# Small products of a two-block transformer kernel, redone: modulation sums, gates, stick-breaking sums, masks and the convolution's norm

## The chip, the cores and the metric

The kernel runs on one core of one Trainium2 chip, in one launch. The metric is the device time of one execution in microseconds (us); lower is better. The median of three runs of the kernel before is 2573.98 us (2573.61 to 2575.96).

The names of the engines below: PE is the matrix engine (PEld its weight loads, which overlap its products), DVE the vector engine, ACT the scalar engine, POOL the general-purpose engine whose queue also issues DMAs, SP the engine whose queue issues the weight loads from DRAM.

## The reference, cut to what matters

256 tokens, width 2048, float32. A first block has two layers: a stick-breaking attention of 16 heads, and a latent attention of 16 heads with a mask by chunks of 64 tokens; each is followed by a per-layer embedding with a gate. A second block is modulated by a vector `c`: a convolution branch with a layer norm, a sparse attention that picks keys, and a feed-forward part of width 5632.

```python
# stick-breaking attention, per head: z [queries, keys]
log_keep = jnp.where(strict, jax.nn.log_sigmoid(-z), 0.0)
later = lax.cumsum(log_keep, axis=3, reverse=True) - log_keep
w = jnp.where(strict, jnp.exp(jax.nn.log_sigmoid(z) + later), 0.0)

# latent attention, per head
s = jnp.where(kchunk[None, :] <= qchunk[:, None], s, NEG_INF)

# second block
mod = silu(c) @ w_ada + b_ada                     # [2048] @ [2048, 12288]
sh1, sc1, gt1, sh2, sc2, gt2 = jnp.split(mod, 6)
x = x + gt1 * rms_norm_2(mixed, g_post_mix)       # later gt2 with g_post_ffn
# in the convolution branch, over 1024 features of each token
y = (xf - mu) * lax.rsqrt(var + EPS)
```

## The kernel before

**The main stream.** Nearly all work is `act @ w` for 256 tokens. The weights come from DRAM in pieces of 512 KB (`Run.load`, tile `wst`, four of them, SP's queue). `Run.consume` splits each piece into two float32r parts, `wh` on ACT (L148) and `wl` on DVE (L149), in a ring of six. `Run.go` then emits, chunk by chunk, three float32r products into `acc` or `sc` (L268 to L270), most of them 512 columns wide. A unit is one piece against one half of the tokens: 6 products of 512 columns.

**Side work.** Everything else is written as generators. After each unit `Run.side` advances those that are due; `yield n` means "n units later". Each engine takes its instructions in the order in which this one program emits them, so the numbers behind `yield` set how far ahead of the matrix engine the other engines get a step. Behind the side work of a unit, `Run.pump` emits the split of the next pieces, at most ten units ahead of their use and only as ring slots are given back by PE.

**Modulation.** `w_ada` is 2048 x 12288. It comes as 384 chunks of 128 x 512 (tile `ast`, three of them, POOL's queue, L245), spread over the whole program. DVE multiplies each by a column of `silu(c)` and adds it to an accumulator `ada` [128, 512] (L421, L424). When 16 chunks are in, `ada_sum` adds up the 128 partitions: four float32 products with a column of ones, one per 128 columns (L435), which put the sums straight into four columns of `tp`; DVE adds the bias into `mods` (L438). There are 24 such sums. A float32 product shows as two passes in the trace, so one sum is 8 passes.

**Gates.** `times_gate` makes gate rows on all partitions: for each of 16 blocks of 128 columns a float32 product of a broadcast column with the identity (L452), and DVE multiplies a row of gains by it (L455). It runs at the start of the mix's output projection (`begin_m`) and, in four pieces, behind the last sum.

**Stick-breaking head.** `stick_head` emits the scores `z` with two float32 products and two masks (bf16 identity times `stick`, 128 columns each), then |z|, exp, ln on ACT and `sp = softplus(z)` on DVE (L646). Three units later three float32 products with triangular or all -1 matrices form the cumulative sums (256, 128 and 128 columns, L634, 6 passes), ACT takes exp into `w`, and two units later the products with `v` follow. All products of this function carry the line L634, that of its helper `mm`.

**Latent head.** `mla_head` (products at L984) adds two bf16 masks of 128 columns, one between the float32 products and one behind them.

**Convolution's norm.** `conv_norm` sums 1024 features per token with a matrix of 1/1024: eight float32 products of 256 columns for the mean (L1165) and, after squares on ACT, eight for the variance (L1179), the latter in four visits.

## Time and profile before

| | |
|---|---|
| median of three runs | 2573.98 us (2573.61 to 2575.96) |
| span of the profiled execution, first to last instruction | 2573.5 us |
| profiled execution's own time | not given apart from the span; the median lies 0.5 us above the span |
| PE busy | 2530.5 us, 98% of the span |
| DVE busy | 1689.0 us, 66% |
| ACT busy | 1262.0 us, 49% |
| POOL busy | 291.8 us, 11% |
| DMA | 562.39 MB, mean 219 GB/s |

A matrix product's record is longer than the time that it takes from the engine, since products are pipelined: the time it takes is the distance from its start to the next one's start. In a timeline an entry with x8 merges eight records, and the next entry's start minus its own is what all eight take. "Idle before" names what released an engine. In the view of waits a row reads: engine, tile and line that waited, the engine, tile and line (or DMA) that ended it, then total us, times, longest.

### The profile page before, as it was taken

What the parts mean: (1) busy time and instruction counts of PE and PEld (TensorE: products, weight loads), DVE (VectorE), ACT (ScalarE), POOL (GpSimd) and SP (SyncE); (2) the same over time, 40 slices, a digit from 0 to 9 for tenths busy, and PEclk for the clock granted to TensorE, in tenths of its full rate; (3) what the DMA queues carried; (4) which work ended last, traced back from release to release, by engine and by line L of the source; (5) the groups of instructions that cost most, each with busy time, mean ns of one, the idle gap of its engine ahead of it and who ended that gap; (6) DMA issues with size and microseconds to landing.
All of it is one profiled execution on the core that took longest, in us unless ns stands there. A gap on an engine that the chain in (4) does not pass through costs nothing.

```text
span 2573.5 us, 33331 instructions
## 1 busy us (share of the span) xinstructions
PE 2530.5 (98%) x12127; PEld 2101.4 (82%) x12127; DVE 1689.0 (66%) x2304; ACT 1262.0 (49%) x1814; POOL 291.8 (11%) x561
## 2 busy tenths in 40 slices
PE   8999999999999999999999999999999999999998
PEld 6888888878889978878877877888788888888886
DVE  6666667677775566668889756676765555645545
ACT  6544464455656545554444554445544444334443
POOL 2111112111313310000000001110100100100000
PEclk9999999999999999999999999999999999999999
DMA  8777768867886566655655535875577777756553
GB/s 266 248 254 250 237 227 283 286 199 247 283 285 191 188 227 208 222 191 174 188 160 168 172 138 181 279 281 197 185 263 232 237 234 233 246 181 188 192 192 127
DMA packets 271844, 562.39 MB, mean 219 GB/s; under 512 B 20800, under 2 KB 43584, under 8 KB 269632
## 3 DMA queue, kind: packets, MB, share of 16 engines
q1 hardware_dynamic: 237264, 439.61, 52.7%
q0 software_dynamic: 34384, 120.65, 13.5%
q8 instruction: 95, 1.56, 0.2%
q14 instruction: 69, 0.57, 0.1%
q10 hardware_dynamic: 32, 0.01, 0.0%
HBM read 551.79 MB, written 8.39 MB: 218 GB/s over the span
## 4 chain that ended last, share of the span: by engine, by line
PE 93%; DVE 4%; ACT 2%; issue 1%; DMA 1%; POOL 0%; DVEq 0%; POOLq 0%; ACTq 0%; SPq 0%
PE acc L268 21%; PE acc L270 21%; PE acc L269 21%; PE sc L268 7%; PE sc L270 7%; PE sc L269 7%; PE tp L363 1%; DVE wl L149 1%; PE sc L634 1%; PE sc L984 1%; PE tp L435 1%; PE sc L1274 1%; PE sc L1240 1%; PE pv L1274 0%; PE tp L610 0%
## 5 line engine op out<-in xcount | busy, mean ns | idle before, releaser
L149 DVE TENSOR_TENSOR wl<-wst,wh 128x1024 fp32r<-128x1024 f32 (+3 forms) x794 | 949.4, 1199 | 628.7 <-ACT wh L148 627.0
L148 ACT ACTIVATE wh<-wst 128x1024 fp32r<-128x1024 f32 (+3 forms) x794 | 822.5, 1039 | 852.5 <-PE sc L270 491.2
L268 PE MATMUL acc<-wh,ah 128*128 128x512 f32 (+4 forms) x1934 | 761.5, 394 | 7.7 <-ACT wh L148 3.7
L269 PE MATMUL acc<-wl,ah 128*128 128x512 f32 (+4 forms) x1934 | 744.6, 385 | 0.9 <-DVE wl L149 0.9
L270 PE MATMUL acc<-wh,al 128*128 128x512 f32 (+4 forms) x1934 | 744.9, 385 | 0.0
L268 PEld LDWEIGHTS acc<-wh,ah 128*128 128x128 f32 x1934 | 365.1, 189 | 81.5 <-issue 6.7
L270 PEld LDWEIGHTS acc<-wh,al 128*128 128x128 f32 x1934 | 364.5, 188 | 72.3 <-DVE al L389 0.9
L269 PEld LDWEIGHTS acc<-wl,ah 128*128 128x128 f32 x1934 | 365.2, 189 | 67.3 <-DVE wl L149 2.5
L245 POOL DMA_DIRECT2D ast<-in_w_ada_dram x384 | 209.3, 545 | 1579.1 <-DVE ada L424 1391.8
L424 DVE SCALAR_TENSOR_TENSOR ada<-ast,silu_c,ada 128x512 f32<-128x512 f32 x360 | 268.7, 746 | 41.3 <-DMA ast<-in_w_ada_dram 40.5
L268 PE MATMUL sc<-wh,ah 128*128 128x512 f32 x538 | 211.5, 393 | 0.0
L270 PE MATMUL sc<-wh,al 128*128 128x512 f32 x538 | 209.6, 390 | 0.0
L269 PE MATMUL sc<-wl,ah 128*128 128x512 f32 x538 | 209.4, 389 | 0.0
L270 PEld LDWEIGHTS sc<-wh,al 128*128 128x128 f32 x538 | 101.0, 188 | 21.4
L268 PEld LDWEIGHTS sc<-wh,ah 128*128 128x128 f32 x538 | 101.0, 188 | 20.5
L269 PEld LDWEIGHTS sc<-wl,ah 128*128 128x128 f32 x538 | 101.1, 188 | 20.3
L1145 DVE SCALAR_TENSOR_TENSOR cv<-cv,wdw 128x255 f32<-128x255 f32 (+14 forms) x240 | 112.4, 468 | 6.5
L153 ACT ACTIVATE wh<-wst,cols 128x512 fp32r<-128x512 f32 (+2 forms) x112 | 68.5, 664 | 47.5 <-PE acc L270 30.5
L154 DVE SCALAR_TENSOR_TENSOR wl<-wst,cols,wh 128x512 fp32r<-128x512 f32 (+2 forms) x112 | 71.3, 681 | 25.5 <-ACT wh L153 25.3
L268 PE MATMUL acc<-wh,hh 128*128 128x512 f32 x176 | 69.3, 393 | 0.0
L268 PE MATMUL sc<-wh,hh 128*128 128x512 f32 x176 | 69.1, 392 | 0.0
L270 PE MATMUL acc<-wh,hl 128*128 128x512 f32 x176 | 68.6, 390 | 0.0
(354 smaller groups left out, 2899.1 us busy)
## 6 DMA issues: line engine op xcount, KB each, us to landing
ast<-in_w_ada_dram POOLq DMA_DIRECT2D x384, 256.0 KB, 4.2
wst<-in_w_in_dram SPq DMA_DIRECT2D x144, 512.0 KB, 3.6
wst<-in_w_in_a_dram SPq DMA_DIRECT2D x120, 512.0 KB, 4.4
wst<-in_w_gate_dram SPq DMA_DIRECT2D x88, 512.0 KB, 4.3
wst<-in_w_up_dram SPq DMA_DIRECT2D x88, 512.0 KB, 4.2
wst<-in_w_down_dram SPq DMA_DIRECT2D x88, 512.0 KB, 4.1
wst<-in_w_ple_gate_dram SPq DMA_DIRECT2D x64, 512.0 KB, 4.8
wst<-in_w_in_b_dram SPq DMA_DIRECT2D x40, 512.0 KB, 4.6
```

The lines of the kernel that those rows point to most:

```text
L148: nc.scalar.activation(wh, st, AF.Copy)
L149: nc.vector.tensor_sub(wl, st, wh.bitcast(F32))
L153: nc.scalar.activation(wh[:, c, :], st[:, c, :], AF.Copy, scale=g)
L154: nc.vector.scalar_tensor_tensor(wl[:, c, :], st[:, c, :], g, wh[:, c, :].bitcast(F32), op0=ALU.mult, op1=ALU.subtract)
L245: self.nc.gpsimd.dma_start(st, x[1])
L268: nc.tensor.matmul(o, lhsT=hi, rhs=wh[:, c, :], start=kc == 0, stop=False)
L269: nc.tensor.matmul(o, lhsT=hi, rhs=wl[:, c, :], start=False, stop=False)
L270: nc.tensor.matmul(o, lhsT=lo, rhs=wh[:, c, :], start=False, stop=kc == b.cp * b.np - 1)
L363: nc.tensor.transpose(tp[:, c * P : (c + 1) * P], src[:, c * P : (c + 1) * P], ident)
L424: nc.vector.scalar_tensor_tensor(acc, w, s, acc, op0=ALU.mult, op1=ALU.add)
L435: nc.tensor.matmul(tp[:, c : c + 1], lhsT=acc[:, c * P : (c + 1) * P], rhs=ones, start=c == 0, stop=True, skip_group_check=True)
L1145: nc.vector.scalar_tensor_tensor(acc[:, sft:], u[:, : S - sft], wdw[:, c, k : k + 1], acc[:, sft:], op0=ALU.mult, op1=ALU.add)
```

## The change

1. `ada_sum`: the accumulator is split into two float32r parts per half (`adh` on ACT, `adl` on DVE, 256 columns), and two float32r products with a [128, 128] matrix of ones put the sum on every partition; ACT copies one row back. Two halves, so two visits of two products per sum. The row of 512 sums goes to DRAM (POOL's queue). After four rows, 16 x 128 come back from DRAM (POOL's queue, four units later) and five units later a transpose of 16 rows makes the 16 columns of `mods`.
2. Gates: for parts 2 and 5 the gains (now columns in `gpost`) are multiplied in on DVE, transposed, copied by ACT and written to DRAM; `row_tile(gate_row(n))` loads the row broadcast to all partitions. `times_gate` is gone, and `begin_f` no longer loads a row.
3. `stick_head`: softplus is kept in `e`, split into `sph` (ACT, with a factor -1) and `spl` (DVE); the sums are four float32r products, two of 384 columns with a triangular matrix and two of 128 columns with the ones. `w` shares the tile `e`.
4. Masks: one bf16 product of 2 x 128 columns per head in place of two of 128, in `stick_head` and `mla_head`.
5. `conv_norm`: DVE adds the eight feature chunks in pairs down to two ahead of the mean (three adds of 512 columns) and the squares (one copy, three adds); two products each remain.
6. Smaller: `masks` live in a temporary tile, `outmask` and `neg_one` are gone (`top_keys` scales `chunk` in the add), `tri`, `ones_r` and `gpost` are made at the start with two more small loads on POOL's queue and one more transpose.

```diff
 def ada_sum(q):
-    yield 6
+    yield 3
     acc = ada_acc.pop(q)
+    for n in range(2):
+        sl = slice(n * 256, n * 256 + 256)
+        hi, lo = (main.tile([P, 256], F32R, tag=f"ad{y}", bufs=1, name=f"ad{y}") for y in "hl")
+        nc.scalar.activation(hi, acc[:, sl], AF.Copy)
+        nc.vector.tensor_sub(lo, acc[:, sl], hi.bitcast(F32))
+        yield 2
+        tp = psum_t()
+        nc.tensor.matmul(tp[:, :256], lhsT=ones_r, rhs=hi, start=True, stop=False)
+        nc.tensor.matmul(tp[:, :256], lhsT=ones_r, rhs=lo, start=False, stop=True)
+        nc.scalar.activation(acc[0:1, sl], tp[0:1, :256], AF.Copy)
+        yield 1
+    row = acc[0:1, :]
+    i, part = q // 4, q % 4
+    if part == 0:
+        mod_rows[i] = dram.tile([16, P], F32, name=f"mod{i}")
+    nc.gpsimd.dma_start(mod_rows[i][4 * part : 4 * part + 4, :].rearrange("(o k) p -> o (k p)", o=1), row)
+    if part < 3:
+        return
+    yield 4
+    m = acc[:16, 0:P]
+    nc.gpsimd.dma_start(m, mod_rows[i])
+    yield 5
     tp = psum_t()
-    for c in range(4):
-        nc.tensor.matmul(tp[:, c : c + 1], lhsT=acc[:, c * P : (c + 1) * P], rhs=ones, ...)
-    sl = slice(q * 4, q * 4 + 4)
-    nc.vector.tensor_tensor(mods[:, sl], tp[:, :4], bcols[:, sl], op=ALU.add)
-    if q == 23:
+    nc.tensor.transpose(tp[:, :16], m, ident[:16, :16])
+    nc.vector.tensor_tensor(mod(i), tp[:, :16], bcols[:, 16 * i : 16 * i + 16], op=ALU.add)
+    if i in (2, 5):
+        g = small(const, 16, "gate")
+        n = i // 3
+        nc.vector.tensor_tensor(g, mod(i), gpost[:, 16 * n : 16 * n + 16], op=ALU.mult)
         yield 2
-        yield from times_gate(st["gp"], 5)
+        tp = psum_t()
+        nc.tensor.transpose(tp[:16, :P], g, ident)
+        gr = acc[:16, P : 2 * P]
+        nc.scalar.activation(gr, tp[:16, :P], AF.Copy)
+        gate_rows[n] = dram.tile([16, P], F32, name=f"gate{n}")
+        nc.gpsimd.dma_start(gate_rows[n], gr)
+    if i == 5:
+        yield 3
+        st["gp"] = row_tile(gate_row(1))
...
 def stick_head(j, h, pv):
-    mm(z[:, 0:128], ident_b, stick)
-    mm(z[:, 256:384], ident_b, stick)
+    mm(diagonal(z), ident_b, both(stick))
...
-    sp = ph.tile([P, 384], tag="sp", bufs=2)
-    nc.vector.scalar_tensor_tensor(sp, z[:, :384], 0.0, e, op0=ALU.max, op1=ALU.add)
+    nc.vector.scalar_tensor_tensor(e, z[:, :384], 0.0, e, op0=ALU.max, op1=ALU.add)
+    parts = [ph.tile([P, 384], F32R, tag=f"sp{y}") for y in "hl"]
+    nc.scalar.activation(parts[0], e, AF.Copy, scale=-1.0)
+    nc.vector.scalar_tensor_tensor(parts[1], e, -1.0, parts[0].bitcast(F32), op0=ALU.mult, op1=ALU.subtract)
     yield 3
-    mm(z[:, 0:256], neg_u, sp[:, 0:256])
-    mm(z[:, 128:256], neg_one, sp[:, 256:384])
-    mm(z[:, 256:384], neg_u, sp[:, 256:384])
-    w = ph.tile([P, 384], tag="w", bufs=2)
+    for y in parts:
+        nc.tensor.matmul(z[:, :384], lhsT=st["tri"], rhs=y, ...)
+    for y in parts:
+        nc.tensor.matmul(z[:, 128:256], lhsT=ones_r, rhs=y[:, 256:384], ...)
+    w = e
...
 def mla_head(j, h, pv):
-    mm(s[:, 0:128], ident_b, chunk)
     mm(s[:, 128:384], qT[:, h, 128:256], kT[:, h, :])
     mm(s[:, 128:384], qT[:, 2, 128:256], krT)
-    mm(s[:, 256:384], ident_b, chunk)
+    mm(diagonal(s), ident_b, both(chunk))
...
 def conv_norm():
-    for c in range(8):
-        nc.tensor.matmul(mu[:, :S], lhsT=mean_c, rhs=acc[:, c, :], start=c == 0, stop=c == 7)
+    nc.vector.tensor_tensor(q2, acc[:, 0:2, :], acc[:, 2:4, :], op=ALU.add)
+    for c0 in (4, 6):
+        nc.vector.tensor_tensor(q2, q2, acc[:, c0 : c0 + 2, :], op=ALU.add)
+    yield 1
+    for i in range(2):
+        nc.tensor.matmul(mu[:, :S], lhsT=mean_c, rhs=q2[:, i, :], start=i == 0, stop=i == 1)
...
 def begin_m():
-    st["gp"] = row_tile(a["g_post_mix_2"])
-    run.finish(run.add(times_gate(st["gp"], 2)))
+    st["gp"] = row_tile(gate_row(0))
 def begin_f():
-    st["gp"] = row_tile(a["g_post_ffn_2"])
```

How the instructions stand, at three places. First PE, at the first modulation sum in the stretch of stick-breaking: four products with the column of ones between two units before,

```order
L270 MATMUL acc<-wh,al 128x512
L435 MATMUL tp<-ones,ada 128x1 x4
L268 MATMUL acc<-wh,ah 128x512
L269 MATMUL acc<-wl,ah 128x512
L270 MATMUL acc<-wh,al 128x512
```

and now, for the first half of the sum:

```order
L270 MATMUL acc<-wh,al 128x512
L445 MATMUL tp<-adh,ones_r 128x256
L446 MATMUL tp<-adl,ones_r 128x256
L268 MATMUL acc<-wh,ah 128x512
L269 MATMUL acc<-wl,ah 128x512
L270 MATMUL acc<-wh,al 128x512
```

One visit of four narrow products became two visits of two products of 256 columns; the second visit stands 18 main products (three units) further down.

Second ACT, at a stick-breaking head (`e` to L644 or L678 are the softplus's steps, `wh` the split of the main stream's weights), before

```order
L642 ACTIVATE e<-sc 128x384
L643 ACTIVATE e<-e 128x384
L644 ACTIVATE e<-e 128x384
L148 ACTIVATE wh<-wst 128x1024
L652 ACTIVATE w<-sc 128x384
```

and now:

```order
L676 ACTIVATE e<-sc 128x384
L677 ACTIVATE e<-e 128x384
L678 ACTIVATE e<-e 128x384
L681 ACTIVATE sph<-e 128x384
L148 ACTIVATE wh<-wst 128x1024
L690 ACTIVATE e<-sc 128x384
```

A copy that needs DVE's softplus came between the logarithm and the next weight split.

Third POOL, in the same stretch, where before one row stood for 127 loads of chunks,

```order
L561 TENSOR_SCALAR rqa_482<-rstd_487 128x1
L245 DMA ast<-in_w_ada_dram 128x512 x127
L504 DMA big<-in_norm_post_dram 128x2048
L718 DMA x<-in_x_dram 128x2048 x2
L800 DMA nat<-in_p_dram 128x256 x2
```

and now, around the third and fourth part of the first of the six rows (`mod` is the table in DRAM):

```order
L453 DMA mod_996<-ada 16x1x32
L245 DMA ast<-in_w_ada_dram 128x512 x16
L453 DMA mod_996<-ada 16x1x32
L245 DMA ast<-in_w_ada_dram 128x512 x2
L458 DMA ada<-mod_996 16x128
L245 DMA ast<-in_w_ada_dram 128x512 x14
L453 DMA mod_2800<-ada 16x1x32
```

Every 16 chunk loads a write of 2 KB, and after every fourth write a read of 8 KB, entered the queue that loads the chunks.

## Rows read from the trace of the kernel before

**Rows 1.** The page's head and the first line of its part 1: busy us, share of the span, instructions.

```profile
span 2573.5 us, 33331 instructions
PE 2530.5 (98%) x12127; PEld 2101.4 (82%) x12127; DVE 1689.0 (66%) x2304; ACT 1262.0 (49%) x1814; POOL 291.8 (11%) x561
```

**Rows 2.** The view of waits, whole program, of all engines and of PE alone: who waited <- for whom: us in total, times, longest.

```profile
POOL ast L245 <- DVE ada L424: 1391.8, 302, 405.4
ACT wh L148 <- PE sc L270: 491.2, 305, 3.5
ACT wh L148 <- DMA wst<-in_w_in_dram: 20.4, 13, 4.4
...
PE tp L1056 <- DVE nat L1407: 5.1, 2, 3.2
...
PE tp L610 <- ACT nat L603: 0.2, 1, 0.2
```

**Rows 3.** Groups of instructions of PE by line and shape: passes | busy us, mean ns of one | idle before.

```profile
L435 PE MATMUL tp<-ones,ada 128*128 128x1 f32 x192 | 22.7, 239 | 0.0
L452 PE MATMUL tp<-ident,mods 128*128 128x128 f32 x64 | 8.1, 276 | 0.0
...
L1165 PE MATMUL pv<-cv,mean_c 128*128 128x256 f32 x16 | 3.6, 379 | 0.0
```

**Rows 4.** Timeline of PE around one modulation sum: start us, us, engine, line, operation.

```profile
90.38 0.95 PE L435 MATMUL tp<-ones,ada 128*128 128x1 f32 x8
...
91.19 0.49 PE L268 MATMUL acc<-wh,ah 128*128 128x512 f32 x1
...
91.51 0.40 PE L269 MATMUL acc<-wl,ah 128*128 128x512 f32 x1
...
91.75 0.40 PE L270 MATMUL acc<-wh,al 128*128 128x512 f32 x1
```

**Rows 5.** Timeline of PE where `begin_m` expands the first gate.

```profile
1739.99 3.89 PE L452 MATMUL tp<-ident,mods 128*128 128x128 f32 x32
1743.63 0.47 PE L268 MATMUL sc<-wh,ah 128*128 128x512 f32 x1
```

**Rows 6.** Timeline of PE in the stretch of latent attention: two main products of 256 columns that follow each other.

```profile
821.48 0.28 PE L270 MATMUL acc<-wh,ckvl 128*128 128x256 f32 x1
821.60 0.28 PE L268 MATMUL acc<-wh,ckvh 128*128 128x256 f32 x1
```

**Rows 7.** Timeline of PE with the transposes of 31 rows at the start (`w_dw`).

```profile
29.72 0.43 PE L587 MATMUL tp<-ident,nat 31*128 31x31 f32 x4
30.08 0.50 PE L268 MATMUL acc<-wh,ah 128*128 128x512 f32 x1
30.41 0.39 PE L269 MATMUL acc<-wl,ah 128*128 128x512 f32 x1
```

**Rows 8.** Groups of ACT and DVE by line and shape, columns as in rows 3.

```profile
L652 ACT ACTIVATE w<-sc 128x384 f32<-128x384 f32 x16 | 7.9, 493 | 36.3 <-PE sc L634 36.3
...
L389 DVE TENSOR_TENSOR al<-tp,ah 128x256 fp32r<-128x256 f32 x16 | 6.0, 420 | 19.3 <-ACT ah L387 19.3
```

**Rows 9.** Timeline of PE at the sums of one stick-breaking head.

```profile
106.88 0.59 PE L634 MATMUL sc<-sp,masks 128*128 128x256 f32 x2
107.31 0.38 PE L634 MATMUL sc<-sp,neg_one 128*128 128x128 f32 x2
107.53 0.39 PE L634 MATMUL sc<-sp,masks 128*128 128x128 f32 x2
107.67 0.48 PE L268 MATMUL acc<-wh,ah 128*128 128x512 f32 x1
```

**Rows 10.** Timelines of DVE and PE from a head's softplus to its sums, for the first head and for the last.

```profile
96.65 0.56 DVE L646 SCALAR_TENSOR_TENSOR sp<-sc,e 128x384 f32<-128x384 f32 x1 [1.46 <-ACT e L644]
...
98.97 0.59 PE L634 MATMUL sc<-sp,masks 128*128 128x256 f32 x2
...
358.39 0.70 PE L634 MATMUL sc<-sp,masks 128*128 128x256 f32 x2 [0.27 <-DVE sp L646]
```

**Rows 11.** Timeline of PE in a latent head: a mask between float32 products.

```profile
808.18 0.22 PE L984 MATMUL sc<-chunk,ident_b 128*128 128x128 bf16 x1
808.23 0.65 PE L984 MATMUL sc<-kT,qT 128*128 128x256 f32 x2
```

**Rows 12.** Timelines of PE and DVE at the convolution's mean.

```profile
1430.02 2.35 DVE L149 TENSOR_TENSOR wl<-wst,wh 128x1024 fp32r<-128x1024 f32 x2
1432.22 3.62 PE L1165 MATMUL pv<-cv,mean_c 128*128 128x256 f32 x16
1435.49 0.58 PE L268 MATMUL acc<-wh,ah 128*128 128x512 f32 x1
1435.91 0.40 PE L269 MATMUL acc<-wl,ah 128*128 128x512 f32 x1
1436.30 1.29 DVE L1170 TENSOR_TENSOR cv<-cv,mus 128x512 f32<-128x512 f32 x2 [1.56 <-ACT mus L1168]
```

**Rows 13.** The view of DMA issues: tensor, queue, count, KB each, median us from issue to landing.

```profile
ast<-in_w_ada_dram POOLq DMA_DIRECT2D x384, 256.0 KB, 4.2
...
nat<-in_kv_latent_norm_dram POOLq DMA_DIRECT2D x1, 2.0 KB, 5.5
```

More of the change, by code (lines that the diff above doesn't have):

```diff
@@ L299, in body @@
     ident = const.tile([P, P], F32, name="ident")
-    masks = const.tile([P, 3, P], F32, name="masks")
-    neg_u, stick_f, chunk_f = (masks[:, i, :] for i in range(3))
     ropes = const.tile([P, 2, 2, 64], F32, name="ropes")
@@ L329, in psum_s, with diagonal, both @@
         return psum.tile([P, NB], F32, tag="sc", bufs=2, name="sc")
+    def diagonal(z):
+        return z.rearrange("p (a b) -> p a b", a=2)[:, :, 0:128]
+    def both(m):
+        return m[:, None, :].to_broadcast([P, 2, P])
     def psum_v():
@@ L443, in mod, with gate_row @@
+        if i == 5:
+            yield 3
+            st["gp"] = row_tile(gate_row(1))
+    mod_rows, gate_rows = {}, {}
+    def gate_row(n):
+        return gate_rows[n].rearrange("(o k) p -> o (k p)", o=1)
     def mod(i):
         return mods[:, 16 * i : 16 * i + 16]
-    def times_gate(g, i):
-        for q in range(4):
-            tp = psum_t()
-            for c in range(4):
-                k = 4 * q + c
-                nc.tensor.matmul(tp[:, c * P : (c + 1) * P], lhsT=mod(i)[:, k : k + 1].to_broadcast([P, P]),
-                                 rhs=ident, start=c == 0, stop=True, skip_group_check=True)
-            sl = slice(q * NB, (q + 1) * NB)
-            nc.vector.tensor_tensor(g[:, sl], tp, g[:, sl], op=ALU.mult)
-            yield 1
@@ L516, in begin_a @@
         rr = nat_tile()
-        rows, brows, rows0 = rr[:112, 0:P], rr[:96, P : 2 * P], rr[:16, 2 * P : 3 * P]
+        rows, brows, rows0, rows1 = rr[:112, 0:P], rr[:96, P : 2 * P], rr[:16, 2 * P : 3 * P], rr[:32, 3 * P :]
         nc.scalar.dma_start(rows0, a["norm_pre0"].rearrange("o (k p) -> (o k) p", p=P))
@@ L527, in begin_a @@
         run.start()
+        masks = nat_tile()[:, : 3 * P].rearrange("p (s n) -> p s n", s=3)
+        neg_u, stick_f, chunk_f = (masks[:, i, :] for i in range(3))
         nc.gpsimd.dma_start(masks, a["k_square"][1:4].rearrange("s p n -> p s n"))
@@ L573, in rest @@
             nc.vector.tensor_copy(chunk, chunk_f)
-            nc.vector.tensor_scalar(outmask, chunk_f, OUT_MASK / NEG, None, op0=ALU.mult)
+            st["tri"] = ph.tile([P, P], F32R, tag="tri")
+            nc.scalar.activation(st["tri"], neg_u, AF.Copy, scale=-1.0)
+            nc.vector.tensor_scalar(ones_r, neg_u, 0.0, 1.0, op0=ALU.mult, op1=ALU.add)
             tp = psum_t()
@@ L577, in rest @@
             nc.tensor.transpose(tp[:, 112:208], brows, ident[:96, :96])
+            nc.tensor.transpose(tp[:, 208:240], rows1, ident[:32, :32])
             nc.vector.tensor_copy(cols[:, 16:], tp[:, :112])
             nc.vector.tensor_copy(bcols, tp[:, 112:208])
+            nc.vector.tensor_copy(gpost, tp[:, 208:240])
             nc.scalar.activation(silu_c, cols[:, GC["c"] : GC["c"] + 16], AF.Silu)
@@ L1173, in conv_norm @@
         var = psum_v()
+        sq = None
         for c0 in range(0, 8, 2):
@@ L1176, in conv_norm @@
             nc.scalar.activation(q.rearrange("p (c n) -> p c n", c=2), acc[:, c0 : c0 + 2, :], AF.Square)
-            yield 2
-            for i in range(2):
-                nc.tensor.matmul(var[:, :S], lhsT=mean_c, rhs=q[:, i * S : (i + 1) * S], start=c0 + i == 0,
-                                 stop=c0 + i == 7)
+            yield 1
+            if sq is None:
+                sq = st["uT"][:, 0:2, :].rearrange("p c n -> p (c n)")
+                nc.vector.tensor_copy(sq, q)
+            else:
+                nc.vector.tensor_tensor(sq, sq, q, op=ALU.add)
+        yield 1
+        for i in range(2):
+            nc.tensor.matmul(var[:, :S], lhsT=mean_c, rhs=sq[:, i * S : (i + 1) * S], start=i == 0, stop=i == 1)
         v, y = (ph.tile([P, 384], tag="pT", bufs=2)[:, :S] for _ in range(2))
@@ L1256, in top_keys @@
         for sl in (slice(0, 128), slice(256, 384)):
-            nc.vector.tensor_tensor(sc[:, sl], sc[:, sl], outmask, op=ALU.add)
+            nc.vector.scalar_tensor_tensor(sc[:, sl], chunk, OUT_MASK / NEG, sc[:, sl], op0=ALU.mult, op1=ALU.add)
         for i in range(8):
```

16 lines of the change are left out of this document (9 added, 7 removed).

## The prediction

> **What bounds the kernel now.** I read the page's busy shares first: PE is busy 98% of a span of 2573.5 us, DVE 66%, ACT 49%, POOL 11% [rows 1]. A busy PE need not be PE at its peak, so the second view is that of waits [rows 2]: ACT stands 491 us (305 times) in front of the weight split for products of PE on `sc` alone, and only 20 us for weights from DRAM on the largest row of that kind. So the weights are split as fast as PE gives ring slots back: supply waits for PE. PE's own largest wait in the same view is 5.1 us. The third view is PE's timeline, read by distances of starts: main products of 512 columns follow each other at 0.23 to 0.24 us (91.51 to 91.75) [rows 4], of 256 columns at 0.12 us [rows 6]. PE works through its list without gaps, so every pass taken from it, or put on it, moves the end by its own length, wherever it stands, until another engine is late at that place. That is the whole method here: price the passes, then look for places where the new steps are late.
>
> The profile's span is 2573.5 us and the median of the runs 2573.98, 0.5 us more. I take the terms from the profile and subtract them from the median.
>
> **The modulation sums.** A visit of 8 passes takes 91.19 - 90.38 = 0.81 us, and the main product behind it 91.51 - 91.19 = 0.32 in place of 0.23, an entry price of 0.09 us when PE comes back from float32 to float32r [rows 4]. 192 passes are 24 visits [rows 3], so 24 x 0.90 = 21.6 us go. What comes: 24 x 2 visits of two float32r products of 256 columns. The same shape in the main stream takes 0.12 us each [rows 6], and no format changes on the way in or out, so 48 x 0.24 = 11.5 us. The trace has no such visit, so the bounds are 0.24 and 0.24 + 0.09 (the entry price of rows 4), that is 11.5 to 15.8; I take the low end, since the row of 256 columns is the same kind of product and format. Six transposes of 16 rows come too. The nearest are four of 31 rows: 30.08 - 29.72 = 0.36, then 0.33 in place of 0.23, so 0.46 for four, entry included [rows 7]; one alone lies between a quarter of the 0.36 (0.09) and 0.46. I take 0.3, x6 = 1.8 us (0.5 to 2.8). Two gate transposes at 0.11 + 0.09 (a pass of 128 columns as in rows 9, and the entry) are 0.4. Net gain 21.6 - 11.5 - 1.8 - 0.4 = 7.9 us.
>
> The visits of few rows are where the trace shows a cost that the column count does not: PE is slow to come back from 31-row operands [rows 7]. The Trainium skill, "TensorEngine Tiling (Array Packing)", section Tiling Modes, states that a change of tiling mode drains the engine, which speaks against the 16-row transposes that the change brings in. The trace is in line with it (0.33 in place of 0.23 us behind the 31-row visit), though float32 visits of all 128 rows show nearly the same 0.32 [rows 4, 7]. By the rule the six cost up to 0.46 each, without it the passes alone, 0.09: 2.8 against 0.5 us of the total, inside the bounds that the rows give.
>
> New waits of these visits: ACT must copy 256 columns and DVE subtract them (0.42 us [rows 8]) in the two units, 12 x 0.23 = 2.7 us, between the emission and PE's products. The nearest row is a step with the same two units, ACT's copy ahead of the transposes of L610: PE waited once, 0.2 us [rows 2]. Here one more engine lies in the chain, behind a weight split of 1.2 us on DVE (half of 2.35 [rows 12]). I take 1 us in all; the bounds are 0 and 48 x 0.2 = 10. Behind the waiting PE stands the main stream itself, so a wait here is paid in full. ACT and DVE themselves have the time: 24 x 2 copies and subtractions and 48 row copies of about 0.4 us, some 60 us on engines that are idle for 900 and more [rows 1].
>
> **The gates.** The first expansion holds PE from 1739.99 to 1743.63, 3.64 us for 32 passes [rows 5], plus the entry 0.09, 3.7; the other 32 of the 64 passes [rows 3] stand in four visits of 8 passes, each as long as a modulation visit, 0.90 [rows 4]: 3.6. Gain 7.3 us. The rows now come broadcast from DRAM, as the gain rows did before; the load stands as early in POOL's queue as the old one, and POOL had run ahead of PE there. Behind the last sum the row is needed at the very end of the feed-forward part, far away. Cost nothing; if the first row were late it would cost a landing, 5.5 us by the slow row of 2 KB [rows 13].
>
> **Stick-breaking sums.** A head's visit is 107.67 - 106.88 = 0.79 us [rows 9], plus the entry 0.09: 16 heads, 14.1 us. It becomes two float32r products of 384 columns (1.5 x 0.12 = 0.18 each [rows 6]) and two of 128. For those the trace has no row; they lie between half of 0.12, by columns, and 0.11, the distance of float32 passes of 128 columns (107.31 to 107.53 for two) [rows 6, 9]. I take 0.11, the pass with the same weight load: 0.58 per head, 9.3 us. Gain 4.8 us (3.4 if the entry is paid, 6.4 at 0.06). The chain behind it grows: after the softplus, ACT copies (0.49 us, the same shape as L652 [rows 8]) and DVE subtracts (0.56, as L646 [rows 10]), with handoffs some 1.1 us. At the first head DVE ends at 97.21 and PE comes at 98.97, 1.76 us later [rows 10]: covered. At the last head PE already waits for DVE (0.27 us [rows 10]), so there the 1.1 us are paid, and what ACT has queued behind its copy (the next weight split and the exp of the weights) is late with it. I take 2 us (1 to 3).
>
> **Masks.** One product of 2 x 128 columns streams as many columns as two of 128; the pass between float32 products takes 0.05 us [rows 11]. I take no gain; the bounds are 0 and 32 x 0.05 = 1.6 us.
>
> **The convolution's norm.** 16 passes take 1435.49 - 1432.22 = 3.27, and the entry is 0.42 - 0.23 = 0.19 [rows 12]: 3.46, or 0.216 a pass. The variance has 16 more (the same eight products by the code), so 6.9 us become 8 passes, 1.7. Gain 5.2 us. The wait: DVE's three adds of 0.65 us (1.29 for two of the same shape) stand behind two weight splits that end at 1432.37, so they end at 1434.3; PE comes one unit (1.4 us) after 1432.22, at 1433.6, and waits 0.7 [rows 12]. At the variance the last add stands one unit ahead in the same way; I add 0.3. Net 4.2 us.
>
> **The start.** A transpose, two loads and two small DVE steps more while the pipeline fills: 0.3 us lost (0 to 1).
>
> **Sum.** 7.9 + 7.3 + 4.8 + 5.2 = 25.2 us gained on PE; 1 + 2 + 1.0 + 0.3 = 4.3 lost to waits and the start. 21 us net: 2573.98 - 21 = 2553 us.
>
> **Rivals.** (a) The passes leave and nothing waits: float32r of 128 columns at 0.06, masks gain, waits at their low ends: 25.2 + 1.6 + 1.6 - 1.7 = 27 less, 2547. For it: the weight supply runs well ahead of PE [rows 2].
>
> (b) The new visits pay the entry price (48 x 0.09 + 16 x 0.09 = 5.8) and the two-engine chain ahead of them is late by 0.1 us a visit (4.8): 10 us less gain, 2563. For it: every visit that the trace shows pays an entry [rows 4, 7, 12]. Against it: all of those change the format.
>
> (c) Slower: the round trips through DRAM starve DVE. POOL's queue is in order; a write waits for ACT's row copy, a read for the write's landing, and the chunk loads stand behind both. DVE, in order too, would stand before its next chunk, and the weight splits behind that; PE runs dry. It decides once a hold lasts longer than the three chunk buffers and the weight ring reach. Each of the 30 holds would have to cost PE over 0.7 us to eat the 21; at a landing of 5.5 us [rows 13] less some 4 that buffers cover, 1.5 us x 30 = 45, 2598. Against it: POOL stands 1392 us waiting for DVE to free a buffer [rows 2], so chunks are loaded well ahead, and a load lands in 4.2 us [rows 13]. The Trainium skill, "SBUF — State Buffer", section "SBUF: two separate sides", speaks for it: a DMA from the GpSimd queue can't write its descriptors while DVE holds the port pair that the two share. If the 34 new DMAs each waited so, they would wait for an instruction of DVE, 1.2 us at most here [rows 12], which POOL's idle time covers; no run here shows such a hold by itself.
>
> (d) Nothing: PE is not the bound and the gain turns into waits for weights, 2573. Against it: rows 2.
>
> **Chances.** The forecast 0.71, (a) 0.10, (b) 0.12, (c) 0.04, (d) 0.03. The range reaches from (a) to (b), with the unknown prices inside: 2546 to 2564. Within 0.2% (5.1 us, about what a measurement of this kernel can tell from no change) lie (d) and a tail of (b): 0.05. Faster 0.91, slower 0.04.
>
> **What would show it.** In the changed kernel's trace: modulation visits at 0.24 us with no entry behind them (0.33 with it); stick visits at 0.58 (0.49 with the cheaper pass of 128 columns); one wait of PE for `spl` at the last head; a wait of about 0.7 us for the adds at the mean; no wait of DVE for chunks beyond the few there are. PE's busy time should fall by about 21 to 25 us. I would be wrong if PE's waits grow by more than 10 us, or if the clock falls behind one of them.

## The result, and the profile after

The changed kernel takes 2560.89 us in the median of four runs (2559.99 to 2564.19), against 2574.97 of the kernel before in the same session: a ratio of 0.9948, 95% interval 0.9934 to 0.9962. It is 14 us faster where 21 were predicted; the time lies inside the range, 8 us above the forecast. The profiled execution took 2564.19 us with a span of 2562.1, the slowest of the four, so its trace accounts for 11.4 us less span than before.

Head of the page, answering to [rows 1], and the waits of PE, answering to [rows 2] (who waited <- for whom: us in total, times, longest):

```profile
span 2562.1 us, 33064 instructions
PE 2509.3 (98%) x11888; PEld 2075.3 (81%) x11888; DVE 1709.3 (67%) x2350; ACT 1299.0 (51%) x1929; POOL 309.9 (12%) x595
```

```profile
PE tp L446 <- DVE adl L442: 4.1, 3, 2.5
...
PE tp L367 <- DVE wide L726: 2.1, 1, 2.1
...
PE sc L685 <- ACT sph L681: 1.5, 1, 1.5
...
PE pv L1208 <- DVE nat L1205: 1.1, 1, 1.1
...
PE tp L445 <- ACT adh L441: 0.9, 1, 0.9
...
PE tp L470 <- DVE gate L467: 0.7, 1, 0.7
```

PE's busy time fell by 21.2 us, but six kinds of waits stand there that the kernel before did not have, or had at 0.5 us (the transposes of `wide`) and 0.3 (the last head's softplus); they are 10.4 us together, 9.6 more than these two.

**The passes.** PE's timeline at a half of a modulation sum, at a transpose of 16 rows, and at the sums of a stick-breaking head (start us, us, engine, line, operation), answering to [rows 4, 7, 9]:

```profile
90.09 0.29 PE L445 MATMUL tp<-adh,ones_r 128*128 128x256 f32 x1
...
90.34 0.39 PE L268 MATMUL acc<-wh,ah 128*128 128x512 f32 x1
90.57 0.40 PE L269 MATMUL acc<-wl,ah 128*128 128x512 f32 x1
...
482.37 0.39 PE L270 MATMUL acc<-wh,bl 128*128 128x512 f32 x1
482.69 0.23 PE L461 MATMUL tp<-ident,ada 16*128 16x16 f32 x1
482.85 0.50 PE L268 MATMUL sc<-wh,bh 128*128 128x512 f32 x1
483.19 0.40 PE L269 MATMUL sc<-wl,bh 128*128 128x512 f32 x1
```

```profile
99.55 0.33 PE L685 MATMUL sc<-sph,tri 128*128 128x384 f32 x1
...
99.89 0.22 PE L687 MATMUL sc<-sph,ones_r 128*128 128x128 f32 x1
99.95 0.28 PE L687 MATMUL sc<-spl,ones_r 128*128 128x128 f32 x1
100.07 0.45 PE L268 MATMUL acc<-wh,ah 128*128 128x512 f32 x1
100.35 0.40 PE L269 MATMUL acc<-wl,ah 128*128 128x512 f32 x1
```

A pair of the sum takes 90.34 - 90.09 = 0.25 us, and the main product behind it 0.23: no entry price. A head's sums take 0.52, and the product behind them 0.28 in place of 0.23: 0.57 in all, 0.58 was predicted. The transpose takes 0.16, but the main product ahead of it 0.32 in place of 0.23 and the one behind it 0.34: 0.36 each.

**Where the time went.** Both traces hold the same 10,368 main products (L268 to L270) in the same order. So I set the start of each one after against its start before; where the difference grows or shrinks, time was lost or gained. It is +0.8 us at the first product and -12.4 at the last, and the part behind the last is 1.0 us longer.

| stretch of the changed kernel | start after minus start before, at its two ends | what lies there |
|---|---|---|
| 8 to 350 us | +0.8 to -6.3 | sums of the modulation and the stick-breaking heads |
| 350 to 405 us | -6.3 to +0.4 | the last head, with a modulation sum on it |
| 405 to 690 us | +0.4 to +0.1 | sums, less a wait of 0.9 at 607 us |
| 690 to 705 us | +0.1 to +3.3 | one modulation sum |
| 705 to 1425 us | +3.3 to +0.8 | sums and masks, less 0.7 at the first gate |
| 1425 to 1462 us | +0.8 to -3.1 | the convolution's norm |
| 1462 us to the end | -3.1 to -12.4 | gates (-3.6 and -3.6), sums |

The gain comes as evenly as predicted, but two stretches of 70 us together give 10 us back. PE's timeline there:

```profile
353.16 0.45 PE L685 MATMUL sc<-sph,tri 128*128 128x384 f32 x1 [1.46 <-ACT sph L681]
...
356.67 0.39 PE L445 MATMUL tp<-adh,ones_r 128*128 128x256 f32 x1 [0.86 <-ACT adh L441]
...
369.83 1.08 PE L367 MATMUL tp<-ident,wide 128*128 128x128 f32 x4 [2.13 <-DVE wide L726]
370.56 0.78 PE L268 MATMUL acc<-wh,ah 128*128 128x512 f32 x1
371.14 0.63 PE L269 MATMUL acc<-wl,ah 128*128 128x512 f32 x1
371.56 0.63 PE L270 MATMUL acc<-wh,al 128*128 128x512 f32 x1
...
690.19 0.39 PE L446 MATMUL tp<-adl,ones_r 128*128 128x256 f32 x1 [2.54 <-DVE adl L442]
```

Behind the two longest waits the main products follow each other at 0.43 us, not at 0.23. The windows of these two stretches (us, busy time and instructions of PE, PEld, DVE, ACT and POOL, then the granted clock, DMA share, GB/s):

```profile
370.56:373.25 2.69, 2.69 (x9) 2.13 (x8) 2.27 (x3) 0.60 (x1) 0.56 (x2) 0.51 1.00 309
690.64:694.05 3.41, 3.41 (x9) 2.62 (x8) 3.41 (x7) 1.88 (x4) 0.55 (x1) 0.50 1.00 349
```

The granted clock is 0.50, the 1.2 GHz level, while PE stands in no further wait. Six products from 370.56 take 2.69 us where the kernel before took 1.48 for them, and the four transposes ahead of them 0.73 in place of 0.35: 1.6 us lost beside the wait of 2.13. Eight products from 690.64 take 3.41 in place of 1.84: again 1.6.

Why was DVE late? Its timeline ahead of each wait; its stand for the second chunk in the kernel before; its waits for chunks in all; and POOL's timeline ahead of the first wait:

```profile
367.19 0.75 DVE L428 SCALAR_TENSOR_TENSOR ada<-ast,silu_c,ada 128x512 f32<-128x512 f32 x1 [2.91 <-DMA ast<-in_w_ada_dram]
...
369.00 0.69 DVE L726 TENSOR_TENSOR wide<-wide,nat 128x512 f32<-128x512 f32 x1
...
681.95 0.75 DVE L428 SCALAR_TENSOR_TENSOR ada<-ast,silu_c,ada 128x512 f32<-128x512 f32 x1 [4.08 <-DMA ast<-in_w_ada_dram]
```

```profile
682.23 0.75 DVE L424 SCALAR_TENSOR_TENSOR ada<-ast,silu_c,ada 128x512 f32<-128x512 f32 x1 [3.70 <-DMA ast<-in_w_ada_dram]
```

```profile
DVE ada L428 <- DMA ast<-in_w_ada_dram: 63.9, 36, 4.8
```

```profile
359.91 0.51 POOL L453 DMA_DIRECT2D mod<-ada  x1 [13.41 <-ACT ada L447]
363.28 1.63 POOL L245 DMA_DIRECT2D ast<-in_w_ada_dram  x3 [2.87 <-DVE ada L428]
```

At 370 us the cause is a hold: POOL stood 13.41 us in front of the write of a sum's row until ACT had copied it; the next chunk loads went out at 363.28, and DVE, in order, stood for a chunk before it came to `wide`. The view of the chain that ended last goes the same way there: 13.40 us of POOL from 346.50 on, then the landing of the load of 363.28.

At 690 us DVE also stood for a chunk, 4.08 us at 682; before, it stood there 3.70 us, and PE did not notice, since the old sum needed the last chunk alone from DVE. The new one needs `adl` too, and from 681.95 to its start at 689.72 DVE works without a pause on what is queued ahead of it, 7.8 us. In all, DVE waits 63.9 us for chunks (36 times), where the kernel before waited 40.5 (32 times).

**The end.** The 1.0 us behind the last product are no chance of one execution: from the start of that product to the end it is 14.0 to 14.3 us in all kernels here with the new modulation, and 13.0 in the kernel before and in e4, which has the old one. What differs is the longest of the three instructions DRAIN of POOL that close the program; it ends 0.8 us ahead of the program's end (how many, ns least/median/most, first start and last end in us; the kernel before, then the changed one):

```profile
L1568 POOLq DRAIN  x3: 46/93/9189, 2563.5 to 2573.2; - x3
L1615 POOLq DRAIN  x3: 46/98/10167, 2551.1 to 2561.8; - x3
```

It takes 10.2 us in place of 9.2. The kernels with the longer one issue 461 DMAs from POOL's queue, the other two 427 and 429; that the DMAs are the cause is likely, but no run shows it alone.

### The profile page after: what moved, and what is told of

Same layout as the page of the kernel before. It is cut to its first block, busy times and chain, and to the rows that moved or that the text cites. A ratio compares the mean times of both kernels' runs of the same rounds, so it can differ in the third digit from the quotient of the medians.

```text
span 2562.1 us, 33064 instructions
## 1 busy us (share of the span) xinstructions
PE 2509.3 (98%) x11888; PEld 2075.3 (81%) x11888; DVE 1709.3 (67%) x2350; ACT 1299.0 (51%) x1929; POOL 309.9 (12%) x595
## 4 chain that ended last, share of the span: by engine, by line
PE 88%; DVE 5%; issue 2%; ACT 2%; DMA 1%; POOL 1%; DVEq 0%; POOLq 0%; ACTq 0%; SPq 0%
PE acc L268 20%; PE acc L270 20%; PE acc L269 20%; PE sc L268 7%; PE sc L270 7%; PE sc L269 7%; DVE wl L149 2%; PE tp L367 1%; PE sc L1022 1%; DVE cv L1182 1%; PE sc L1323 1%; PE sc L1289 1%; DMA ast<-in_w_ada_dram 1%; PE pv L1323 0%; PE tp L645 0%
## 5 line engine op out<-in xcount | busy, mean ns | idle before, releaser
L268 PE MATMUL acc<-wh,ah 128*128 128x512 f32 (+4 forms) x1934 | 760.8, 393 | 6.5 <-ACT wh L148 3.8
L270 PE MATMUL acc<-wh,al 128*128 128x512 f32 (+4 forms) x1934 | 745.7, 386 | 0.0
L268 PEld LDWEIGHTS acc<-wh,ah 128*128 128x128 f32 x1934 | 365.8, 189 | 80.1 <-issue 6.7
L270 PEld LDWEIGHTS acc<-wh,al 128*128 128x128 f32 x1934 | 365.0, 189 | 73.0 <-DVE al L393 0.9
L428 DVE SCALAR_TENSOR_TENSOR ada<-ast,silu_c,ada 128x512 f32<-128x512 f32 x360 | 268.2, 745 | 64.4 <-DMA ast<-in_w_ada_dram 63.9
L268 PE MATMUL sc<-wh,ah 128*128 128x512 f32 x538 | 211.2, 393 | 0.0
L270 PE MATMUL sc<-wh,al 128*128 128x512 f32 x538 | 209.5, 389 | 0.0
L270 PEld LDWEIGHTS sc<-wh,al 128*128 128x128 f32 x538 | 101.0, 188 | 21.3
L268 PEld LDWEIGHTS sc<-wh,ah 128*128 128x128 f32 x538 | 101.0, 188 | 20.7
L268 PE MATMUL acc<-wh,hh 128*128 128x512 f32 x176 | 69.1, 392 | 0.0
L268 PE MATMUL sc<-wh,hh 128*128 128x512 f32 x176 | 68.9, 392 | 0.0
L270 PE MATMUL acc<-wh,hl 128*128 128x512 f32 x176 | 68.6, 390 | 0.0
```

What stands on the lines that cost most here:

```text
L268: nc.tensor.matmul(o, lhsT=hi, rhs=wh[:, c, :], start=kc == 0, stop=False)
L270: nc.tensor.matmul(o, lhsT=lo, rhs=wh[:, c, :], start=False, stop=kc == b.cp * b.np - 1)
L428: nc.vector.scalar_tensor_tensor(acc, w, s, acc, op0=ALU.mult, op1=ALU.add)
```

## The experiments

Each kernel ran beside the kernel before; the differences below are between medians, and each ratio is to the kernel before.

**e1: more lead for the split.**

```diff
             nc.vector.tensor_sub(lo, acc[:, sl], hi.bitcast(F32))
-            yield 2
+            yield 5
```

> The changed kernel with one number changed: in the sum of the modulation, five units instead of two between the split of a half (ACT's copy, DVE's subtraction) and its two products. Theory L (the split comes too late because two units are less than what stands on ACT and DVE at a few places): PE's waits for the two parts (4.1 us for the one from DVE, 0.9 for the one from ACT) go, and with the 2.5 us wait at 690 us also the stretch at half clock behind it (about 1.6 us), so 2554 to 2556 us. The wait of 2.1 us of the transposes at 370 us stays. Theory P (the writes to DRAM hold the queue that loads the chunks, so DVE is late with everything): the waits for DVE's part stay or move elsewhere, 2560 to 2562 us.

Measured: 2554.48 us (2552.87 to 2555.63), ratio 0.9920 (0.9906 to 0.9933), 6.4 us less than the changed kernel. The view of waits shows none for `adl` or `adh`, while DVE still stands 62.4 us for chunks. So the lead was the matter, not the chunks as such. One part came out otherwise than expected: the wait at 370 us went as well (0.5 is left). The longer lead also moved the write of that sum behind the chunk loads in POOL's queue, which go out at 356.16 now. By this run alone, the lead and the hold are not told apart at that place.

**e2: the write later, the lead as it was.**

```diff
             nc.scalar.activation(acc[0:1, sl], tp[0:1, :256], AF.Copy)
-            yield 1
+            yield 1 if n == 0 else 5
```

> The changed kernel with one number changed: the row of a sum is written to DRAM five units behind the second pair of products instead of one. Theory P (POOL's queue stands in front of that write until ACT has copied the row, and the chunk loads behind it come late): DVE's idle time for chunks falls from 64 to about 41 us, the level of the kernel before; the wait of 2.1 us of the transposes at 370 us and the half clock behind it (about 1.5 us) go, 2557 us. Theory L (only the lead of the split counts): 2561 us, no change that can be measured.

Measured: 2559.99 us (2556.50 to 2563.08), ratio 0.9940 (0.9928 to 0.9953). In time this can't be told from the changed kernel. In its trace the mechanism of theory P is plain. The waits of DVE for chunks, and POOL's timeline:

```profile
DVE ada L428 <- DMA ast<-in_w_ada_dram: 36.8, 23, 4.7
```

```profile
357.08 0.55 POOL L245 DMA_DIRECT2D ast<-in_w_ada_dram  x1 [11.01 <-issue]
```

The loads go out 6.2 us earlier, DVE stands 27 us less, and the wait at 370 us is gone. POOL stands 11.01 us at this place even without the write ahead of the load, so of the 13.41 us no more than these 6.2 held a load back. The wait for `adl` at 690 us is still there (2.12 us, at 685 in this trace): that one comes from the lead, not from the hold. The profiled execution, with 2556.50 us, was the fastest of the five.

**e3 and e4: the change in two halves.** e3 keeps the modulation, the gates and the masks, and has the float32 sums and the norm of the kernel before:

```diff
-        parts = [ph.tile([P, 384], F32R, tag=f"sp{y}") for y in "hl"]
...
+        mm(z[:, 0:256], st["neg_u"], sp[:, 0:256])
+        mm(z[:, 128:256], st["neg_one"], sp[:, 256:384])
+        mm(z[:, 256:384], st["neg_u"], sp[:, 256:384])
...
+        for c in range(8):
+            nc.tensor.matmul(mu[:, :S], lhsT=mean_c, rhs=acc[:, c, :], start=c == 0, stop=c == 7)
```

> The changed kernel with the stick-breaking sums and the convolution's norm put back (the three float32 products of a head, softplus in a tile of its own; sixteen float32 products of the norm); what stays is the modulation, the gates and the masks. By the terms of the prediction alone: 14 us less than before, 2560 us. By the waits of the changed kernel's trace, if those at 352 to 373 us come from the stick-breaking chain: 16.8 us of passes less 7.5 of waits and start, 9 less than before, 2565 us. If those waits belong to the sum of the modulation that falls on the last head: 2568 to 2569 us.

e4 is the other half, with `ada_sum`, `times_gate` and the loads of the gain rows of the kernel before:

```diff
+        for c in range(4):
+            nc.tensor.matmul(tp[:, c : c + 1], lhsT=acc[:, c * P : (c + 1) * P], rhs=ones, ...)
...
-        st["gp"] = row_tile(gate_row(0))
+        st["gp"] = row_tile(a["g_post_mix_2"])
+        run.finish(run.add(times_gate(st["gp"], 2)))
```

> The changed kernel with the modulation's sum and the gates of the kernel before; what stays is the stick-breaking sums, the norm and the masks. If the waits at 352 to 373 us belong to the sum of the modulation: one wait of about 1.3 us at the last head stays and one of 1.1 at the norm, 11.6 us of passes less 3, so 9 less than before, 2565 us. If the longer chain of a stick-breaking head makes them: 2569 to 2570 us.

Measured: e3 2569.14 us (2565.42 to 2570.84), ratio 0.9974 (0.9965 to 0.9983), 6.0 us less than before. e4 2565.26 us (2564.95 to 2568.63), ratio 0.9966 (0.9953 to 0.9978), 9.9 us less. Together 15.9, of which the masks count twice: the whole change, 14.1. So the halves add up, and the half with the modulation, which was to bring most, brings least. With gates and masks at their prices (7.3 and, by the visits, 2.4 us, see below), the sums of the modulation cost some 3 to 4 us by subtraction (no run has them alone), passes, waits and the longer end together, instead of saving 7.9. The waits after the last head belong to them. In e3's timeline, with the old stick-breaking sums, they stand all the same (`wide` is L723 there):

```profile
360.75 0.38 PE L446 MATMUL tp<-adl,ones_r 128*128 128x256 f32 x1 [0.91 <-DVE adl L442]
...
372.11 0.63 PE L367 MATMUL tp<-ident,wide 128*128 128x128 f32 x4 [1.60 <-DVE wide L723]
```

In e4 only what the longer stick-breaking chain costs by itself is left there (waits of PE; `sph` is L658, the exp of the weights L667):

```profile
PE sc L662 <- ACT sph L658: 0.8, 1, 0.8
PE pv L646 <- ACT e L667: 0.7, 1, 0.7
```

**e5 and e6: a lead at every late place.** e5 has the five units of e1, the later write for three of four rows, four units ahead of the gate's transpose, and two ahead of the mean and the variance; e6 also gives the head's sums four units.

```diff
             nc.vector.tensor_sub(lo, acc[:, sl], hi.bitcast(F32))
-            yield 2
+            yield 5
...
             nc.scalar.activation(acc[0:1, sl], tp[0:1, :256], AF.Copy)
-            yield 1
+            yield 1 if n == 0 or q % 4 == 3 else 5
...
             nc.vector.tensor_tensor(g, mod(i), gpost[:, 16 * n : 16 * n + 16], op=ALU.mult)
-            yield 2
+            yield 4
...
             nc.vector.tensor_tensor(q2, q2, acc[:, c0 : c0 + 2, :], op=ALU.add)
-        yield 1
+        yield 2
...
```

> The changed kernel with more lead at every place where PE newly waited: five units instead of two ahead of each pair of products, the row written four units later for three of the four parts of a row, the gate's transpose four units instead of two behind its product, the convolution's mean and variance two units instead of one behind the adds. Theory (what the change lost beyond its passes are waits for steps that were emitted too late, and the clock that falls behind the longest of them): the lead alone gave 2554.5 us; the wait of 1.1 us at the mean goes too, 2553 to 2554 us, and of the new waits of PE only that for the last stick-breaking head (1.5 us) is left. Rival (the waits only move to the next late step): 2556 to 2561 us.

> The kernel with all leads, and four units instead of three between a stick-breaking head's softplus and its sums. Theory: the wait at the last head (1.5 us) is covered by the 1.4 us of one unit, 2552 us. Rival (the later heads delay the output projection's input, and that wait takes its place): 2554 to 2556 us.

Measured: e5 2552.24 us (2551.52 to 2552.92), ratio 0.9906 (0.9893 to 0.9920), 8.7 us less than the changed kernel. Of the new waits only the one at the last head is left (1.7 us); a wait that the kernel before had at 0.4 us, that of the latent heads' products with `v` for `wide`, is 1.4 here. e6 2551.00 us (2549.59 to 2552.90), ratio 0.9900 (0.9885 to 0.9915): as fast as e5 within what can be told. Its trace shows the rival's trade: the wait for `sph` went, and one for the exp of the weights took its place, 1.9 us where it was 0.5. Both beat both kernels.

**e7: every pair twice**, on e5, to price a pass in place.

```diff
-            nc.tensor.matmul(tp[:, :256], lhsT=ones_r, rhs=hi, start=True, stop=False)
-            nc.tensor.matmul(tp[:, :256], lhsT=ones_r, rhs=lo, start=False, stop=True)
+            for _ in range(2):
+                nc.tensor.matmul(tp[:, :256], lhsT=ones_r, rhs=hi, start=True, stop=False)
+                nc.tensor.matmul(tp[:, :256], lhsT=ones_r, rhs=lo, start=False, stop=True)
```

> The kernel with all leads, with every pair of products of the modulation's sum issued twice (the second pair overwrites the first, the result is the same). If PE's list is the bound everywhere and a pass of 256 columns costs 0.12 us: 96 x 0.12 = 11.5 us more than the kernel with all leads, 2565 us. If the visits carry an entry price, the doubling still adds the passes alone. Rival (the visits partly hide in time that PE loses elsewhere): 0 to 6 us more, 2553 to 2560 us.

Measured: 2561.85 us (2560.94 to 2564.08), ratio 0.9945 (0.9933 to 0.9958), 9.6 us more than e5, 0.10 us for each of the 96 passes: between what the two expectations add (11.5, and 0 to 6), nearer the first. In the timeline a doubled visit shows starts 0.12 apart (93.10, 93.22, 93.35). Passes are paid where they stand; some 2 us of the 11.5 did not come out in the medians.

**e8: the masks put back**, on e5; the same edit as here in a latent head, also in `stick_head`.

```diff
+        mm(s[:, 0:128], ident_b, chunk)
         mm(s[:, 128:384], qT[:, h, 128:256], kT[:, h, :])
         mm(s[:, 128:384], qT[:, 2, 128:256], krT)
-        mm(diagonal(s), ident_b, both(chunk))
+        mm(s[:, 256:384], ident_b, chunk)
```

> The kernel with all leads, with the two mask products of 128 columns of each head as in the kernel before. By the prediction's term (one product of 2 x 128 columns costs what two of 128 cost): no change, 2553 to 2554 us. By the visits of the changed kernel's trace (a latent head's scores 0.10 us shorter with the one product, a stick-breaking head's 0.04): 16 x 0.10 + 16 x 0.04 = 2.3 us more, 2555 to 2556 us; in its trace the visit of a latent head's scores takes 1.44 us again in place of 1.34.

Measured: 2553.68 us (2552.03 to 2556.54), ratio 0.9913 (0.9900 to 0.9927), 1.4 us more than e5: between the two expectations, and not to be told from either in time. The visit tells more. The changed kernel's latent head, and e8's:

```profile
830.97 0.38 PE L1022 MATMUL sc<-kT,qT 128*128 128x128 f32 x2
...
832.30 0.42 PE L268 MATMUL acc<-wh,cqh 128*128 128x384 f32 x1
```

```profile
801.31 0.39 PE L1023 MATMUL sc<-kT,qT 128*128 128x128 f32 x2
...
801.76 0.22 PE L1023 MATMUL sc<-chunk,ident_b 128*128 128x128 bf16 x1
801.81 0.65 PE L1023 MATMUL sc<-kT,qT 128*128 128x256 f32 x2
...
802.76 0.42 PE L268 MATMUL acc<-wh,cqh 128*128 128x384 f32 x1
```

1.33 us against 1.45. The mask between float32 products costs its own 0.05 (801.76 to 801.81), and the float32 pair behind it takes 0.49 (801.81 to 802.30) where it takes 0.43 in the changed kernel (831.41 to 831.84).

**e9: the holds as long as they can be**, on e5: the write right behind ACT's second copy, the read right behind the fourth write.

```diff
-            yield 1 if n == 0 or q % 4 == 3 else 5
+            if n == 0:
+                yield 1
...
-        yield 4
         m = acc[:16, 0:P]
         nc.gpsimd.dma_start(m, mod_rows[i])
-        yield 5
+        yield 9
```

> The kernel with all leads, but with the holds of POOL's queue made as long as the program allows: the row is written right behind ACT's copy of its second half (five units earlier for three parts of four), and the table is read back right behind the fourth write, so that the queue also stands out that write's landing. Theory P (a hold delays chunk loads, DVE stands for them in order, and what DVE owes PE is late): DVE's idle time for chunks rises from 40 us to 65 or more, POOL's hold for the row copy from 88 to over 200 us, and PE gets waits for DVE that the kernel with all leads does not have; 2555 to 2560 us. Rival (with the split emitted five units ahead, DVE's stands for chunks reach nothing that PE waits for): DVE's idle time rises all the same, and the time stays at 2552 to 2553 us.

Measured: 2557.81 us (2555.87 to 2561.43), ratio 0.9935 (0.9922 to 0.9947), 5.6 us more than e5 (7 by the two ratios). Theory P holds, even with the long lead. POOL stands 215.9 us for row copies (88.0 in e5). The waits of DVE for chunks (40.3 in e5), and DVE's timeline at the first place where PE pays:

```profile
DVE ada L428 <- DMA ast<-in_w_ada_dram: 104.7, 48, 7.8
```

```profile
265.49 0.75 DVE L428 SCALAR_TENSOR_TENSOR ada<-ast,silu_c,ada 128x512 f32<-128x512 f32 x1 [5.86 <-DMA ast<-in_w_ada_dram]
```

The late chunk delays the softplus of an ordinary head (267.29), ACT's copy `sph` behind it, and PE waits 1.37 us at 268.45; three waits for `wide` (2.1 us together) follow the same pattern.

**e10: one unit more**, the same place as e1 with `yield 3`.

```diff
-            yield 2
+            yield 3
```

> The changed kernel with one unit (1.4 us) more lead: three units instead of two ahead of each pair of products. Theory L: each wait for a part of the sum gets about 1.4 us shorter, so the 2.5 us wait at 690 us falls to about 1.1 and the stretch at half clock behind it (1.6 us) goes, and the waits under 1.4 us go: about 5 us less than the changed kernel, 2555 to 2557 us. Rival (the waits come from where the sums fall, not from how far ahead the split is): 2559 to 2562 us.

Measured: 2554.06 us (2553.52 to 2558.49), ratio 0.9923 (0.9909 to 0.9936), 6.8 us less than the changed kernel, some more than the 5 expected, and not all of it in the expected way. One wait for `adl` is left, and it is 2.0 us long, not 1.1; the clock fell behind it. The waits at 356 us went, and of that at 370 us 0.3 is left; the chunk load stands ahead of the write in POOL's queue, as in e1. In their place one of 1.3 us came for the exp of the weights at the last head. So theory L's count by units is right for most of the waits and wrong for the one for `adl`, which hangs on when the chunk came.

## Why the prediction was right, and which term was off

**Passes: right.** PE is the bound, and passes taken out are gained (e7: 0.10 to 0.12 us a pass). Modulation sums 7.2 us (7.9 predicted): 24 x 0.90 out, 48 x 0.25 in, six transposes at 0.36 and two gate transposes at 0.11. There the entry price is absent, as taken, the transposes of 16 rows cost more than the 0.3 taken, and those of the gates less than the 0.2. Gates 7.3 as predicted. Stick-breaking sums 5.0 (4.8). Norm 4.9 (5.2). Masks 2.4 by the visits (0 predicted, bound 1.6): 16 x 0.11 and 16 x 0.04; in time e8 shows 1.4, which can't be told from nothing. Sum 26.8 against 25.2.

On the 16-row transposes the rule quoted from the Trainium skill, "TensorEngine Tiling (Array Packing)", section Tiling Modes, that a change of mode drains the engine, fits better than I gave it credit for: a 16-row visit is paid on both sides, 0.32 us ahead and 0.34 behind, while the float32 visits of all rows in the kernel before show the price behind alone. The price ahead stood in that kernel's trace too, at the 31-row transposes of [rows 7], where the prediction counted the price behind only. The products ahead of the 31 rows (next start 29.72) and of a modulation sum (next start 90.38):

```profile
29.40 0.39 PE L270 MATMUL acc<-wh,al 128*128 128x512 f32 x1
...
90.15 0.39 PE L270 MATMUL acc<-wh,al 128*128 128x512 f32 x1
```

0.32 us against 0.23. That a drain is what is paid for, no run shows.

**Waits: mis-sized, and this is the term that was off.** "New waits of these visits ... I take 1 us in all." The waits for `adl`, `adh` and the gate are 5.7 us in the trace, 1.6 us of half clock behind one of them, and the hold at 370 us another 2.1 + 1.6: 11 us, beyond the upper bound of 10. I priced them as an average per visit from one row with ACT alone in the chain. They are not spread like that: of 48 visits three wait for `adl` and one for `adh`: the longest (2.54 us) where DVE has stood for a chunk, two (0.9 each) at the last head, where ACT has five loads of function tables queued, 1.28 us each, and one (0.6, at 1768 us) behind two weight splits. The stand and the loads were in the trace before; I read PE's waits and not what stood in the queues of DVE and ACT at the places where the sums fall. e1 and e5 show it: with more lead these waits go, and 6 to 9 us come back.

**The last head.** 2 us predicted (1 to 3); by e4, 0.8 + 0.7 us at it alone, where the kernel before had 0.3 + 0.2: 1.0 more, the low end. In the whole change a modulation sum falls on it, and the wait is 1.5, followed by the others; it is for `sph` of ACT, not for `spl` as predicted.

**Norm.** 0.7 us at the mean predicted, 1.1 measured; nothing at the variance, where I had added 0.3. **Start.** 0.3 predicted, 1.2 measured (0.8 of it ahead of the first product, a figure that lies between 0.1 and 0.8 in the runs of e1 to e5). At 60 us into the program the start differs by 1.1 here and by -0.2 to 0.8 in e1 to e10, so most of it is chance of the execution. **The end.** Nothing predicted, 1.0 measured, the longer DRAIN.

The terms close to about 1 us: 26.8 us of passes less 11 for the modulation's waits, 1.5 for the last head, 1.1 for the mean, 1.2 for the start, 1.0 for the end and 0.9 at 607 us is 10.1. Waits of the kernel before that are gone give back 2.0 (1.0 for ACT's `wide` of L899, 0.5 for the transposes of `wide`, 0.5 at the last head): 12.1, and the spans differ by 11.4. The median of the changed kernel lies 3.3 us below its profiled execution, hence most of the step to 14.

**The signs named ahead.** Visits of 0.25 and 0.57 us and 21.2 us less busy time came as named. DVE's waits for chunks did not stay: 63.9 us for 40.5. Of the two signs of being wrong, one came: the clock fell behind two of the new waits. The other, PE's waits up by more than 10 us, missed by little (9.6). So the range holds and the passes are right, but the part on waits is not. With the leads of e5 the kernel comes to 2552 us, where the forecast was 2553. That it comes so close is in part luck: the masks gave 2.4 us that were not counted, and the end took 1.0 that was not either.

**Rivals.** (b), 2563, is the nearest in time, half for the wrong reason: no entry was paid, but the chain was late. (c), the hold of POOL's queue, was real: one hold of 13.4 us, 6.2 of it in front of a load that could have gone, cost 3.7 us here, and the longer holds of e9 cost 5.6. What was wrong in (c) is the price of 1.5 us for each of 30 holds. POOL's queue stood 21 times for a row copy, 204 us in all, and behind most of these stands DVE found its chunks loaded (it stood for them 36 times in place of 32). The rule that ACT, DVE and GpSimd take their instructions strictly in order (the Trainium skill, "Perfetto Trace Analysis", section Tensor Engine Instruction (MATMUL, LD_WEIGHTS)) is what the rows at 346 to 370 us show: a write of 2 KB ahead, and loads, sums and transposes late behind it. The hold by the port pair that I quoted for (c) shows in none of the rows read here.

What stays open: how much of the hold's 3.7 us reaches the median of the changed kernel. e2 took it away in the trace and not, as far as can be told, in the median.

## What to carry to other kernels

When a step on a saturated engine is exchanged for one that is cheaper there but needs two other engines first, price the passes from the rows, and then go to each place where the new step falls and read what those engines have queued there: a few late visits, not the average, took 11 of 27 us. Set the lead by the longest backlog, a stand for a DMA included, and not by the work of the step itself. A small DMA that waits for data holds every load behind it on its queue: issue it when its data are surely there.

## What the runs showed of the hardware

PE's clock went to 0.50 behind waits of 2.13 and 2.54 us in the changed kernel and added 1.6 us to each. Behind waits of 0.9 and 1.46 us it did not. Behind one of 2.03 us in e10 it did, and behind one of 2.12 us at the same sum in e2 it did not. PE's timelines, e10 first:

```profile
685.01 0.39 PE L446 MATMUL tp<-adl,ones_r 128*128 128x256 f32 x1 [2.03 <-DVE adl L442]
...
686.33 0.63 PE L269 MATMUL acc<-wl,ah 128*128 128x512 f32 x1
686.76 0.63 PE L270 MATMUL acc<-wh,al 128*128 128x512 f32 x1
```

```profile
685.04 0.39 PE L446 MATMUL tp<-adl,ones_r 128*128 128x256 f32 x1 [2.12 <-DVE adl L442]
...
686.20 0.39 PE L269 MATMUL acc<-wl,ah 128*128 128x512 f32 x1
686.43 0.39 PE L270 MATMUL acc<-wh,al 128*128 128x512 f32 x1
```

0.43 us from product to product in the one, 0.23 in the other. So the same wait costs 2 us in one execution and nearly 4 in another, as much as the difference between some of the kernels here. One more wait shows it, that of a main product for ACT's `wide` (L1328 before, L1377 after) near 1400 us, which all kernels have: the clock fell behind it in e1, e3 and e5 to e9 (1.99 to 2.57 us long), and not in the kernel before, the changed one, e2, e4 and e10 (2.01 to 2.65). The length of a wait alone does not decide.

Of two passes of 128 float32r columns the second starts 0.06 us behind the first (99.89 to 99.95), and the main product 0.12 behind the second (99.95 to 100.07); the pair together is 0.18, between the bounds taken. Why the two differ, no run shows.
